# Third layer norm's factor in tile order and 36 two-operand operations on VectorE instead of GpSimd, in a float32 hybrid decoder block

## The chip, the cores and the metric

The kernel runs on one core of a Trainium2 chip, in one launch. The metric is the device time of that launch in microseconds (us), the median of several runs. Engines are named as in the profile: PE is TensorE (matmuls), DVE is VectorE, ACT is ScalarE, POOL is GpSimd, and SP issues the DMAs.

## What is computed

One layer on x of shape (1, 1024, 1024) in float32: a SwiGLU block with half weight, a token mixer (gated convolution beside an S5 state space), a second SwiGLU block, and a gated embedding, each followed by a layer norm.

```python
x = layer_norm(ALPHA * x + 0.5 * swiglu(x, ffn1_w_in, ffn1_w_out), ln1_g, ln1_b)
x = layer_norm(ALPHA * x + token_mixer(x, ...), ln2_g, ln2_b)
x = layer_norm(ALPHA * x + 0.5 * swiglu(x, ffn2_w_in, ffn2_w_out), ln3_g, ln3_b)
e = (p @ ple_w_in) * sigmoid(x @ ple_w_gate)
x = layer_norm(ALPHA * x + e, ln4_g, ln4_b)
```

Here `swiglu(x, w_in, w_out)` is `(silu(gate) * up) @ w_out` with `gate, up` the halves of `x @ w_in`; D is 1024, the inner width of a SwiGLU block 2816, the embedding 256 wide.

## The kernel before, in words

Every float32 product is made of three matmuls: an operand is split into a high part (a cast to fp32r on ACT, line 175) and a low part (operand minus high part, a two-operand instruction on DVE or POOL, line 176), and high times high, high times low and low times high are summed in PSUM (`pm` banks, six of them). Weights arrive in blocks of 128x512 (`Ws`), and their parts are `Wh` and `Wl`, three buffers each: PE can go on with a block when its `Wl` is written.

The large products are done with Winograd's variant of Strassen: seven products in place of eight. That needs sums of operands: of the activations (t1, t2, t3, t4 from the quarters 11, 12, 21, 22) once per stage, and of the weights for each pair of blocks (`rest`, lines 73 to 103; `s` is made by POOL at lines 79, 84 and 96).

Four places matter here.

- **The start.** `first_operands` (lines 380 to 439) loads x in pieces `xp` of 128x1024 and splits quarters 11 and 21. Its inner function `later` (lines 422 to 438) makes the activations' sums in two halves j = 0, 1: half 0 on DVE, half 1 on POOL, at lines 426, 429, 432 and 437. Each sum is then split (`xt1h`/`xt1l` and so on). Meanwhile PE does the first products of five block pairs (x11, then x21), then those on t1, t2, t3.
- **The two transitions into a Winograd stage**, from the first SwiGLU block into the mixer and from the mixer into the second SwiGLU block. `out_phase` (lines 219 to 237) does the output products (line 229) tile by tile, s = 0 to 7, DVE adds them into `acc` (line 234), and its callback `after(s)` normalizes the tile on DVE (`normalize`, `moments`, lines 241 to 265; the last step, line 265, for six of the eight) and, after every second tile, calls the sink on that pair of tiles. The sink transposes them on PE (line 281, into one of two `pt` banks), applies the norm's factor and offset on ACT (line 283) and makes and splits the sums (`winograd_sink`, lines 340 to 375): at lines 365, 369, 371 and 373 those of half j = 0 on POOL, of half j = 1 on DVE.
- **The transition into the last stage** has the same callback with `plain_sink` (lines 328 to 338), which only splits.
- **The last stage** (lines 1229 to 1259), tile by tile, s = 0 to 7. `apply(acc2[s])` (lines 311 to 316) multiplies a tile by the third norm's factor and adds its offset, columns 0 to 511 on DVE, columns 512 to 1023 on POOL, a product (line 315) and a sum (line 316) each, of 128x512. PE makes the gate's product (line 1243, 24 matmuls per half tile) into `pm` and the embedding's (line 1248, 6 matmuls) into `pt`. ACT takes the sigmoid (line 1251, `sg`), DVE multiplies the embedding's product by it (line 1252, which frees the `pt` bank), adds that to the tile (line 1253), and makes the last norm (lines 1254 to 1258), whose result goes out by DMA.

Who does what when is not written out: the program is recorded in the order of the code, and a scheduler then gives each engine its own queue, an instruction standing where it would have its inputs, earlier code first among those that are ready. Each engine then works through its queue in that order. `tc.issue_after(ins)`, which the change uses, holds what is recorded inside it behind `ins` in the queue of `ins`'s engine.

Of the kernel before, what the change touches and what calls it, by code (L numbers as in the profile page):

```python
# [12 lines left out]
ALU = mybir.AluOpType  # L13
P = 128
# [3 lines left out]
NT = 8  # L18
# [87 lines left out]
class Block:  # L106
# [112 lines left out]
    def out_phase(self, hs, ws, acc, scale, bank, after=None, fresh=False):  # L219
        nc = self.nc  # L220
        n = len(hs)
        for s in range(NT):
            for dh in range(2):
                ps = bank()
                cols = slice(dh * 512, (dh + 1) * 512)
                for j in range(n):
                    (hh, hl), (wh, wl) = hs[j], ws[j]
                    for i, (a, b) in enumerate(((hh, wh), (hh, wl), (hl, wh))):
                        nc.tensor.matmul(ps, a[:, s * P:(s + 1) * P], b[:, cols],  # L229
                                         start=(j == 0 and i == 0), stop=(j == n - 1 and i == 2))  # L230
                if fresh:
# [4 lines left out]
            if after is not None:  # L236
                after(s)

# [62 lines left out]
    def affine(self, g, b, tag):  # L301
# [8 lines left out]

        def apply(t):
            for h in range(2):
                sl = slice(h * 512, (h + 1) * 512)
                eng = (self.nc.vector, self.nc.gpsimd)[h]
                eng.tensor_tensor(t[:, sl], t[:, sl], gb[h], ALU.mult)
                eng.tensor_tensor(t[:, sl], t[:, sl], gb[2 + h], ALU.add)  # L316
        return apply
# [22 lines left out]
    def winograd_sink(self, xs, gb):  # L340
# [9 lines left out]
        def sink(i, pair):  # L350
# [8 lines left out]
            for j in range(2):  # L359
# [3 lines left out]
                self.features(pair, gb, 2 * j, b12)  # L363
                eng = (gps, self.nc.vector)[j]
                eng.tensor_tensor(t1, b12, b11, ALU.subtract)
# [14 lines left out]
    def first_operands(self, xT, w_in):  # L380
# [41 lines left out]
        def later():  # L422
            tt = [self.t("H", [P, 2, 512], name="t1") for _ in range(2)]
            eng = (nc.vector, nc.gpsimd)
            for j in range(2):
                eng[j].tensor_tensor(tt[j], p["12", j], p["11", j], ALU.subtract)
                put("t1", j, tt[j])
            for j in range(2):
                eng[j].tensor_tensor(tt[j], p["22", j], tt[j], ALU.subtract)
                put("t2", j, tt[j])  # L430
            for j in range(2):
                eng[j].tensor_tensor(p["12", j], p["22", j], p["12", j], ALU.subtract)
                put("t3", j, p["12", j])
            for j in range(2):
                put("22", j, p["22", j])
            for j in range(2):
                eng[j].tensor_tensor(tt[j], p["21", j], tt[j], ALU.subtract)
                put("t4", j, tt[j])
# [710 lines left out]
    def run(self, a, out):  # L1149
# [22 lines left out]
        def then(acc, make, sink):  # L1172

            state = {}

            def after(s):
                if s == 0:
                    state["x"] = make()
                    state["sink"] = sink(state["x"])
                self.normalize(acc[s], s < 2)  # L1180
                if s % 2:
                    state["sink"](s // 2, acc[s - 1:s + 1])
            return state, after
# [40 lines left out]
        for v in ("ln4_g", "ln4_b"):  # L1224
            for h in range(2):
                tl = self.t("Ws", [P, 512], name="gb4")
                nc.sync.dma_start(tl, a[v][h * 512:(h + 1) * 512].partition_broadcast(P))
                gb4.append(tl)
        for s in range(NT):
            cols = slice((s % 4) * P, (s % 4 + 1) * P)  # L1230
            if s % 2 == 0:
                pp = self.split_w(self.stage(a["pT"][:, s // 2]))
            apply(acc2[s])
            pcol = lambda k: slice((2 * (s % 2) + k) * P, (2 * (s % 2) + k + 1) * P)
            cuts = HALVES if s < NT - 1 else (slice(0, 512), slice(512, 768), slice(768, D))
            for sl in cuts:
# [14 lines left out]
                nc.scalar.activation(sg, pg, AF.Sigmoid)  # L1251
                nc.vector.tensor_tensor(sg, pe, sg, ALU.mult)
                nc.vector.scalar_tensor_tensor(acc2[s][:, sl], sg, 1.0 / ALPHA, acc2[s][:, sl], ALU.mult, ALU.add)
# [68 lines left out]
```

## Time and profile before

| | before |
|---|---|
| median of 3 runs | 2084.79 us (2083.38 to 2086.32) |
| the profiled execution, its own time | 2086.58 us |
| span of the profiled execution | 2084.8 us |
| PE busy | 2001.7 us, 96% of the span |
| DVE busy | 1668.0 us, 80% |
| ACT busy | 813.7 us, 39% |
| POOL busy | 846.4 us, 41% |
| mean granted clock of TensorE | 0.991 |

The span is the time from the first to the last instruction that the profile shows. PE is busy nearly all of it, and the share of an engine is a mean over stages of different kinds; what an edit is worth is read in the stage where it lies, from who waits there for whom. A matmul of 128x512 shows 0.39 us and the next one starts 0.227 us after it at the full clock, so 112 of them are seen in a stretch of 25 us that loses nothing.

### The profile page before, as it was taken

To read this page: it belongs to the slowest core of one execution; us is meant where nothing else is said; L and a number is where in the kernel's file an instruction comes from. 1 tells how busy PE (TensorE), PEld (TensorE's weight loads), DVE (VectorE), ACT (ScalarE), POOL (GpSimd) and SP (SyncE) were. 2 spreads that over 40 slices of the span, in tenths; PEclk is the share of its full clock that TensorE was granted. 3 is DMA by queue.
4 is the path that set the end of the run, shared out by engine and by line. 5 is a ranking of instruction groups with operands and counts; after the bars stand their busy time and mean duration, and the time that the engine had idled before them with its cause. 6 is when DMAs were issued, how large, how long until landed. Compare 5 with 4: busy or idle time off the path is not lost.

```text
span 2084.8 us, 26465 instructions
## 1 busy us (share of the span) xinstructions
PE 2001.7 (96%) x9030; PEld 1633.4 (78%) x9030; DVE 1668.0 (80%) x2560; ACT 813.7 (39%) x1422; POOL 846.4 (41%) x562
## 2 busy tenths in 40 slices
PE   7999999999999899999999999999999999999988
PEld 5887778776788777887878888788888876788867
DVE  7789888879998976767644679877667789998897
ACT  5333343445342545343533415533333345342520
POOL 3644444454313454333201372654444444313360
PEclk9999999999999999999999999999999999999999
DMA  4433343556540264333382410243323246431111
GB/s 170 127 117 96 122 141 126 179 186 223 164 141 25 106 187 148 100 122 114 133 299 80 151 53 17 83 149 117 101 87 126 91 166 217 162 128 69 54 45 69
DMA packets 153238, 260.24 MB, mean 125 GB/s; under 512 B 16144, under 2 KB 61200, under 8 KB 153104
## 3 DMA queue, kind: packets, MB, share of 16 engines
q1 hardware_dynamic: 153104, 258.56, 37.6%
q8 instruction: 71, 1.16, 0.2%
q14 instruction: 63, 0.52, 0.1%
HBM read 189.85 MB, written 68.65 MB: 124 GB/s over the span
## 4 chain that ended last, share of the span: by engine, by line
PE 67%; DVE 21%; issue 5%; DMA 2%; ACT 2%; POOL 2%; SPq 0%; DVEq 0%; POOLq 0%; ACTq 0%
PE pm L198 42%; PE pm L615 11%; PE pm L209 5%; PE pm L229 5%; DVE Wl L176 4%; PE pm L1243 2%; DVE wt L176 2%; DVE w L176 1%; DVE acc L622 1%; DVE ln L254 1%; PE pt L1248 1%; DVE ln L248 1%; DVE ln L255 1%; DVE acc L316 1%; DVE acc L234 1%
## 5 line engine op out<-in xcount | busy, mean ns | idle before, releaser
L175 ACT CAST Wh<-Ws 128x512 fp32r<-128x512 f32 x268 | 166.6, 622 | 346.5 <-PE pm L198 277.5
L176 DVE TENSOR_TENSOR Wl<-Ws,Wh 128x512 fp32r<-128x512 f32 x268 | 212.8, 799 | 109.1 <-ACT Wh L175 108.7
L175 ACT CAST Wh<-s 128x512 fp32r<-128x512 f32 x240 | 149.2, 622 | 379.2 <-PE pm L198 139.3
L176 DVE TENSOR_TENSOR Wl<-s,Wh 128x512 fp32r<-128x512 f32 x240 | 213.5, 890 | 25.8 <-ACT Wh L175 25.7
L615 PE MATMUL pm<-wt,Wh 128*128 128x512 f32 x640 | 188.0, 392 | 2.5 <-DVE acc L622 2.5
L84 POOL TENSOR_TENSOR s<-s,Ws 128x512 f32<-128x512 f32 x60 | 90.2, 1503 | 203.6 <-DVE Wl L176 193.3
L102 POOL TENSOR_TENSOR u<-u,p 128x512 f32<-128x512 f32 x60 | 96.1, 1602 | 144.3 <-DVE u L92 93.2
L615 PE MATMUL pm<-w,Wh 128*128 128x512 f32 x480 | 141.4, 392 | 6.1 <-ACT Wh L175 5.5
L622 DVE SCALAR_TENSOR_TENSOR acc<-pm,acc 128x512 f32<-128x512 f32 x200 | 132.7, 682 | 15.5 <-PE pm L615 14.8
L615 PEld LDWEIGHTS pm<-wt,Wh 128*128 128x128 f32 x640 | 119.7, 188 | 30.2 <-DVE acc L622 3.3
L79 POOL TENSOR_TENSOR s<-Ws 128x512 f32<-128x512 f32 x60 | 82.5, 1374 | 133.8 <-DVE Wl L176 102.0
L96 POOL TENSOR_TENSOR s<-Ws,s 128x512 f32<-128x512 f32 x60 | 92.3, 1538 | 108.8 <-DVE Wl L176 107.4
L615 PE MATMUL pm<-wt,Wl 128*128 128x512 f32 x320 | 113.8, 394 | 3.9 <-DVE Wl L176 3.6
L615 PEld LDWEIGHTS pm<-w,Wh 128*128 128x128 f32 x480 | 90.0, 189 | 26.8 <-ACT Wh L175 7.1
L198 PE MATMUL pm<-x11h,Wh 128*128 128x512 f32 (+1 forms) x264 | 99.1, 384 | 5.0 <-ACT x11h L175 5.0
L198 PE MATMUL pm<-x11h,Wl 128*128 128x512 f32 (+1 forms) x264 | 99.3, 379 | 3.1 <-DVE Wl L176 3.1
L198 PE MATMUL pm<-x11l,Wh 128*128 128x512 f32 (+1 forms) x264 | 99.6, 380 | 1.9 <-DVE x11l L176 1.3
L198 PE MATMUL pm<-xt1h,Wl 128*128 128x512 f32 x240 | 95.3, 397 | 5.3 <-DVE Wl L176 5.3
L198 PE MATMUL pm<-x21h,Wl 128*128 128x512 f32 x240 | 95.1, 396 | 5.5 <-DVE Wl L176 5.5
L198 PE MATMUL pm<-xt2h,Wl 128*128 128x512 f32 x240 | 94.8, 395 | 4.2 <-DVE Wl L176 4.1
L198 PE MATMUL pm<-xt4h,Wl 128*128 128x512 f32 x240 | 94.1, 392 | 4.6 <-DVE Wl L176 4.6
L198 PE MATMUL pm<-xt1l,Wh 128*128 128x512 f32 x240 | 94.4, 393 | 2.1 <-DVE xt1l L176 2.1
(355 smaller groups left out, 5615.7 us busy)
## 6 DMA issues: line engine op xcount, KB each, us to landing
Ws<-in_ffn_w_in SPq DMA_DIRECT2D x196, 256.0 KB, 2.7
Ws<-in_ffn_w_out SPq DMA_DIRECT2D x88, 256.0 KB, 3.1
Ws<-in_w_mix SPq DMA_DIRECT2D x74, 256.0 KB, 2.7
s<-h_s SPq DMA_DIRECT2D x60, 256.0 KB, 3.0
h<-a SPq DMA_DIRECT2D x58, 256.0 KB, 2.3
ha<-h SPq DMA_DIRECT2D x20, 512.0 KB, 4.1
hb<-h SPq DMA_DIRECT2D x20, 512.0 KB, 4.6
h_s<-u SPq DMA_DIRECT2D x20, 256.0 KB, 2.6
```

The costliest lines, as they stand in the source:

```text
L79: gps.tensor_tensor(s, a21, a22, ALU.add)
L84: gps.tensor_tensor(s, s, a11, ALU.subtract)
L96: gps.tensor_tensor(s, a12, s, ALU.subtract)
L102: gps.tensor_tensor(u3, u3, p5, ALU.add)
L175: self.nc.scalar.copy(hi, src)
L176: (lo_eng or self.nc.vector).tensor_tensor(lo, src, hi.bitcast(F32), ALU.subtract)
L198: self.nc.tensor.matmul(ps[:, tok], w[a][:, sl], x[b](k)[:, tok], start=(start and k == 0 and i == 0), stop=(k == nk - 1 and i == 2), skip ...
L209: self.nc.tensor.matmul(ps[h], w[a][:, sl], x(h)[b](k), start=(k == 0 and i == 0), stop=(k == 3 and i == 2))
L229: nc.tensor.matmul(ps, a[:, s * P:(s + 1) * P], b[:, cols], start=(j == 0 and i == 0), stop=(j == n - 1 and i == 2))
L615: nc.tensor.matmul(ps[i], hh[p][:, cols], w[n][:, j, q], start=(start and j == 0 and k == 0), stop=(j == 1 and k == 2), skip_group_check=n ...
L622: vec.scalar_tensor_tensor(t, ps[i], scale, t, ALU.mult, ALU.add)
L1243: nc.tensor.matmul(pg, xx[p](k % 4)[:, cols], wg[dh][k][q][:, col], start=(k == 0 and i == 0), stop=(k == NK - 1 and i == 2))
```

## The change

Four edits. The operands' sums of the start and of `winograd_sink` are all on DVE (4 + 16 instructions leave POOL). `apply` is on DVE alone (16 instructions leave POOL), and it is held, from the second tile on, behind the line 1252 instruction of the tile before. The sink of a pair of tiles is called one tile later, behind that tile's last output matmul on PE; the last pair's is called as before.

```diff
@@ out_phase
-                        nc.tensor.matmul(ps, a[:, s * P:(s + 1) * P], b[:, cols],
+                        mm = nc.tensor.matmul(ps, a[:, s * P:(s + 1) * P], b[:, cols],
...
-                after(s)
+                after(s, mm)
@@ affine
         def apply(t):
+            vec = self.nc.vector
             for h in range(2):
                 sl = slice(h * 512, (h + 1) * 512)
-                eng = (self.nc.vector, self.nc.gpsimd)[h]
-                eng.tensor_tensor(t[:, sl], t[:, sl], gb[h], ALU.mult)
-                eng.tensor_tensor(t[:, sl], t[:, sl], gb[2 + h], ALU.add)
+                vec.tensor_tensor(t[:, sl], t[:, sl], gb[h], ALU.mult)
+                vec.tensor_tensor(t[:, sl], t[:, sl], gb[2 + h], ALU.add)
@@ winograd_sink
-                eng = (gps, self.nc.vector)[j]
+                eng = self.nc.vector
@@ first_operands, later
-            eng = (nc.vector, nc.gpsimd)
+            vec = nc.vector
             for j in range(2):
-                eng[j].tensor_tensor(tt[j], p["12", j], p["11", j], ALU.subtract)
+                vec.tensor_tensor(tt[j], p["12", j], p["11", j], ALU.subtract)
...
@@ run, then
-            def after(s):
+            def after(s, mm):
...
                 self.normalize(acc[s], s < 2)
-                if s % 2:
+
+                if s % 2 == 0 and s:
+                    with self.tc.issue_after(mm.ins):
+                        state["sink"](s // 2 - 1, acc[s - 2:s])
+                elif s == NT - 1:
                     state["sink"](s // 2, acc[s - 1:s + 1])
@@ run, last stage
+        last = None
         for s in range(NT):
...
-            apply(acc2[s])
+
+            with self.tc.issue_after(last.ins) if last else ExitStack():
+                apply(acc2[s])
...
-                nc.vector.tensor_tensor(sg, pe, sg, ALU.mult)
+                last = nc.vector.tensor_tensor(sg, pe, sg, ALU.mult)
```

How the queues move, at three places. The names are those of the words above; a number is a buffer's.

On DVE at the start, from the sum for t1 on (`t_349` is half 0, `t_350` half 1), before:

```order
L426 TENSOR_TENSOR t_349<-xp 128x1024
L176 TENSOR_TENSOR Wl<-Ws,Wh 128x512
L176 TENSOR_TENSOR xt1l<-t_349,xt1h 128x1024
L176 TENSOR_TENSOR Wl<-Ws,Wh 128x512
L176 TENSOR_TENSOR xt1l<-t_350,xt1h 128x1024
L429 TENSOR_TENSOR t_349<-xp,t_349 128x1024
L432 TENSOR_TENSOR xp<-xp 128x1024
L176 TENSOR_TENSOR Wl<-Ws,Wh 128x512
L176 TENSOR_TENSOR xt2l<-t_349,xt2h 128x1024
L176 TENSOR_TENSOR Wl<-Ws,Wh 128x512
```

and now:

```order
L426 TENSOR_TENSOR t_349<-xp 128x1024
L176 TENSOR_TENSOR Wl<-Ws,Wh 128x512
L426 TENSOR_TENSOR t_350<-xp 128x1024
L176 TENSOR_TENSOR xt1l<-t_349,xt1h 128x1024
L176 TENSOR_TENSOR Wl<-Ws,Wh 128x512
L176 TENSOR_TENSOR xt1l<-t_350,xt1h 128x1024
L429 TENSOR_TENSOR t_349<-xp,t_349 128x1024
L432 TENSOR_TENSOR xp<-xp 128x1024
L176 TENSOR_TENSOR Wl<-Ws,Wh 128x512
L429 TENSOR_TENSOR t_350<-xp,t_350 128x1024
L432 TENSOR_TENSOR xp<-xp 128x1024
L176 TENSOR_TENSOR Wl<-Ws,Wh 128x512
```

The three sums of half 1 shown stand between the splits (the fourth, line 437, comes ten rows below); POOL's queue begins with line 79 instead.

On DVE at the beginning of the last stage (`acc_10364` to `acc_10371` are the tiles, `gb_16941` to `gb_16944` the two halves of the factor and of the offset), before, from the eighth product on:

```order
L315 TENSOR_TENSOR acc_10371<-acc_10371,gb_16941 128x512
L316 TENSOR_TENSOR acc_10364<-acc_10364,gb_16943 128x512
L316 TENSOR_TENSOR acc_10365<-acc_10365,gb_16943 128x512
L316 TENSOR_TENSOR acc_10366<-acc_10366,gb_16943 128x512
L1252 TENSOR_TENSOR sg_17057<-pt_17050,sg_17057 128x512
L316 TENSOR_TENSOR acc_10367<-acc_10367,gb_16943 128x512
L316 TENSOR_TENSOR acc_10368<-acc_10368,gb_16943 128x512
L1252 TENSOR_TENSOR sg_17093<-pt_17086,sg_17093 128x512
```

and now, from the first product on (lines are those of the changed kernel: 1252 is 1259 there, 1253 is 1260):

```order
L315 TENSOR_TENSOR acc_10364<-acc_10364,gb_16941 128x512
L315 TENSOR_TENSOR acc_10364<-acc_10364,gb_16942 128x512
L316 TENSOR_TENSOR acc_10364<-acc_10364,gb_16943 128x512
L1259 TENSOR_TENSOR sg_17057<-pt_17050,sg_17057 128x512
L316 TENSOR_TENSOR acc_10364<-acc_10364,gb_16944 128x512
L1260 SCALAR_TENSOR_TENSOR acc_10364<-sg_17057,acc_10364 128x512
L1259 TENSOR_TENSOR sg_17093<-pt_17086,sg_17093 128x512
L315 TENSOR_TENSOR acc_10365<-acc_10365,gb_16941 128x512
L315 TENSOR_TENSOR acc_10365<-acc_10365,gb_16942 128x512
```

Eleven products and sums, over eight tiles, stood ahead of the first line 1252 instruction; three of the first tile stand there now, and the other tiles' follow by turns.

On PE in the transition from the first SwiGLU block into the mixer, at the first transposes (line 281) among the output products, in the changed kernel:

```order
L229 MATMUL pm<-wo,hp 128x512 x43
L281 MATMUL pt<-ident,acc 128x128 x2
L229 MATMUL pm<-wo,hp 128x512 x26
L281 MATMUL pt<-ident,acc 128x128 x6
L229 MATMUL pm<-wo,hp 128x512 x8
L281 MATMUL pt<-ident,acc 128x128 x8
```

These rows are the same in the kernel before. Of each transition's 64 transposes, those of the first three pairs of tiles keep their places in PE's queue; those of the fourth pair move, in the two transitions into a Winograd stage, by up to 24 matmuls.

## Rows read from the trace of the kernel before

**Rows 1.** The page's part 1: engine, busy us, share, instructions.

```profile
PE 2001.7 (96%) x9030; PEld 1633.4 (78%) x9030; DVE 1668.0 (80%) x2560; ACT 813.7 (39%) x1422; POOL 846.4 (41%) x562
```

**Rows 2.** Windows: stretch, length; PE, PEld, DVE, ACT, POOL busy (instructions); clock; DMA, GB/s.

```profile
25.00:50.00 25.00, 18.18 (x64) 13.26 (x63) 25.00 (x16) 14.64 (x19) 15.32 (x6) 0.87 0.14 43
50.00:75.00 25.00, 25.00 (x112) 20.64 (x111) 16.13 (x21) 7.74 (x13) 15.52 (x11) 1.00 0.32 100
725.00:750.00 25.00, 21.07 (x89) 15.03 (x88) 24.41 (x25) 18.29 (x34) 16.16 (x11) 1.00 0.52 150
...
1300.00:1325.00 25.00, 20.95 (x91) 15.56 (x90) 21.31 (x23) 19.97 (x38) 18.37 (x10) 0.97 0.15 43
...
2000.00:2025.00 25.00, 17.70 (x61) 13.97 (x62) 24.93 (x33) 4.13 (x8) 15.88 (x10) 0.80 0.00 0
2025.00:2050.00 25.00, 25.00 (x112) 20.71 (x111) 24.97 (x70) 1.80 (x3) 0.00 (x0) 1.00 0.22 85
```

**Rows 3.** Instructions of one line: duration ns min/median/max, first and last start.

```profile
L365 DVE TENSOR_TENSOR t<-b,y x4: 677/682/687, 714.9 to 1317.0; 128x512 f32<-128x512 f32 x4
L365 POOL TENSOR_TENSOR t<-b,y x4: 1277/1527/1759, 708.1 to 1306.6; 128x512 f32<-128x512 f32 x4
```

**Rows 4.** The same view of line 315 in the last stage.

```profile
L315 DVE TENSOR_TENSOR acc<-acc,gb x8: 1684/1776/1780, 1986.1 to 1997.9; 128x512 f32<-128x512 f32 x8
```

**Rows 5.** Timeline of DVE at the start: start us, us, instruction, [idle before].

```profile
16.95 3.49 DVE L426 TENSOR_TENSOR t<-xp 128x1024 f32<-128x1024 f32 x1
...
24.65 1.22 DVE L429 TENSOR_TENSOR t<-xp,t 128x1024 f32<-128x1024 f32 x1
...
45.52 0.68 DVE L176 TENSOR_TENSOR Wl<-s,Wh 128x512 fp32r<-128x512 f32 x1
```

**Rows 6.** Timeline of POOL at the start.

```profile
46.27 2.19 POOL L84 TENSOR_TENSOR s<-s,Ws 128x512 f32<-128x512 f32 x1 [4.03 <-DVE Wl L176]
```

**Rows 7.** Timeline of PE at the start.

```profile
46.25 0.50 PE L198 MATMUL pm<-xt1h,Wl 128*128 128x512 f32 x1 [3.20 <-DVE Wl L176]
...
51.17 0.39 PE L198 MATMUL pm<-xt2h,Wl 128*128 128x512 f32 x1
```

**Rows 8.** Timelines of POOL, ACT and DVE in the two transitions into Winograd stages.

```profile
716.84 7.09 POOL L371 TENSOR_TENSOR t<-b,t 128x512 f32<-128x512 f32 x1 [3.84 <-DVE xt1l L176]
723.88 1.29 POOL L79 TENSOR_TENSOR s<-Ws 128x512 f32<-128x512 f32 x1
...
723.96 1.02 ACT L283 ACTIVATE b<-pt,gbT 128x256 f32<-128x256 f32 x2 [2.71 <-POOL t L371]
...
725.52 1.57 DVE L176 TENSOR_TENSOR Wl<-Ws,Wh 128x512 fp32r<-128x512 f32 x1 [2.74 <-ACT Wh L175]
...
1297.58 6.48 POOL L371 TENSOR_TENSOR t<-b,t 128x512 f32<-128x512 f32 x1 [5.07 <-DVE xt1l L176]
```

**Rows 9.** Waits of PE, us in total, times, longest: 715 to 750; then 1283 to 1345.

```profile
PE pm L198 <- DVE Wl L176: 3.5, 4, 1.4
...
PE pm L198 <- DVE Wl L176: 3.8, 3, 2.3
PE pm L198 <- DVE xt1l L176: 1.8, 1, 1.8
```

**Rows 10.** Timelines of DVE and PE at the beginning of the last stage.

```profile
1986.06 13.54 DVE L315 TENSOR_TENSOR acc<-acc,gb 128x512 f32<-128x512 f32 x8 [1.19 <-DMA gb<-in_ln_g]
1999.53 5.08 DVE L316 TENSOR_TENSOR acc<-acc,gb 128x512 f32<-128x512 f32 x3
2004.53 0.68 DVE L1252 TENSOR_TENSOR sg<-pt,sg 128x512 f32<-128x512 f32 x1
...
2005.27 1.22 PE L1248 MATMUL pt<-wp,Wh 128*128 128x512 f32 x2 [7.14 <-DVE sg L1252]
2016.14 1.07 PE L1248 MATMUL pt<-wp,Wh 128*128 128x512 f32 x2 [2.03 <-DVE sg L1252]
```

**Rows 11.** Groups of DVE from 2023 to 2050 us: busy us, mean ns.

```profile
L1257 DVE SCALAR_TENSOR_TENSOR acc<-acc,ln,gb 128x512 f32<-128x512 f32 x8 | 5.8, 743 | 0.0
```

More of the change, by code (lines that the diff above doesn't have):

```diff
@@ L228, in out_phase @@
                     for i, (a, b) in enumerate(((hh, wh), (hh, wl), (hl, wh))):
-                        nc.tensor.matmul(ps, a[:, s * P:(s + 1) * P], b[:, cols],
-                                         start=(j == 0 and i == 0), stop=(j == n - 1 and i == 2))
+                        mm = nc.tensor.matmul(ps, a[:, s * P:(s + 1) * P], b[:, cols],
+                                              start=(j == 0 and i == 0), stop=(j == n - 1 and i == 2))
                 if fresh:
@@ L423, in later @@
             tt = [self.t("H", [P, 2, 512], name="t1") for _ in range(2)]
-            eng = (nc.vector, nc.gpsimd)
+            vec = nc.vector
             for j in range(2):
-                eng[j].tensor_tensor(tt[j], p["12", j], p["11", j], ALU.subtract)
+                vec.tensor_tensor(tt[j], p["12", j], p["11", j], ALU.subtract)
                 put("t1", j, tt[j])
             for j in range(2):
-                eng[j].tensor_tensor(tt[j], p["22", j], tt[j], ALU.subtract)
+                vec.tensor_tensor(tt[j], p["22", j], tt[j], ALU.subtract)
                 put("t2", j, tt[j])
             for j in range(2):
-                eng[j].tensor_tensor(p["12", j], p["22", j], p["12", j], ALU.subtract)
+                vec.tensor_tensor(p["12", j], p["22", j], p["12", j], ALU.subtract)
                 put("t3", j, p["12", j])
@@ L436, in later @@
             for j in range(2):
-                eng[j].tensor_tensor(tt[j], p["21", j], tt[j], ALU.subtract)
+                vec.tensor_tensor(tt[j], p["21", j], tt[j], ALU.subtract)
                 put("t4", j, tt[j])
```

## The prediction, made before the changed kernel had run

> **What bounds the kernel now.** I read the shares first, then windows, then PE's waits, then timelines of whoever PE waits for. The shares show PE busy 96% of the span and POOL under half [rows 1]; PE decides, so only places where PE loses time count. A stretch of 25 us that loses nothing holds 112 full matmuls, one every 0.227 us (25/112). In the windows the reader should see four places that hold fewer [rows 2]: 64 at the start, 89 in the transition into the mixer, 91 in the next Winograd transition, 61 in the last stage; in all four DVE is busy 21 to 25 of 25 us. That is 10.9, 5.2, 4.8 and 11.6 us lost ((112 − n) × 0.227). All four are places of the change.
>
> Why is DVE late there? The same line and shape takes 0.68 us on DVE and 1.28 to 1.76 on POOL in a transition [rows 3], and 1.78 on DVE while POOL does the same work beside it [rows 4]. A 128x1024 sum takes 3.49 us beside POOL and 1.22 without [rows 5]. The two engines lengthen each other. Successive DVE instructions overlap by 0.08 us (eight shown as 13.54 us from 1986.06, the next at 1999.53 [rows 10]), so undisturbed ones cost **0.60** (512 columns) and **1.14** (1024).
>
> **The change, part by part.** Thirty-six instructions go from POOL to DVE: 4 of 1024 columns, 16 and 16 of 512. Undisturbed they add 4 × 1.14 + 32 × 0.60 = 23.8 us to DVE; the question is what the others get shorter by.
>
> *A, start.* PE's products on t1 wait 3.20 us, until 46.25, for the `Wl` that DVE writes last in a queue of splits and sums [rows 5, 7]. From the first sum (16.95) to the end of that `Wl` (46.2) DVE took 29.3 us. Its queue there, after the change, holds 15 instructions of 1024 columns and 6 of 512: 15 × 1.14 + 6 × 0.60 = 20.7 us. Three of the 15 are new, so the old queue was worth 17.3 and lost 12 us to POOL and to waits. POOL keeps two of the weights' sums in that time; one beside DVE took 2.19 [rows 6], and I let the pair cost DVE 2.2, with 1.1 for short waits: 16.95 + 24.0 = 41.0, 5.2 earlier. Three more instructions of 1024 (half 1 of t4, its splits) and three of 512 stand before t2's `Wl`: 41.0 + 3 × 1.14 + 3 × 0.60 = 46.2, where PE began t2's low part at 51.17 [rows 7]. **A = 5.0 us.** Low end 2, if POOL's remaining sums and waits take 6.5 in place of 3.3; high end 8.5, if neither costs anything (16.95 + 20.7 = 37.7). What is late next is PE itself, with the products on x21 still to do.
>
> *B, two Winograd transitions.* Eight sums each go to DVE, 8 × 0.60 = 4.8 us. Into the mixer POOL's t3 sum stood 7.09 us; ACT waited 2.71 for it, then DVE 2.74 for ACT's `Wh` [rows 8]: DVE, which PE waits for, was itself waiting for POOL. On DVE this sum costs 0.60 and the chain is gone, at 4.8 us of DVE work of which 2.74 fits in that wait. PE waited 3.5 us for `Wl` and lost 5.2 in the window [rows 9, 2]: **B1 = 3.5**, between 0 (the added work eats it) and 5.2. In the next transition the sum stood 6.48 [rows 8]; PE waited 3.8 for `Wl` and 1.8 for the t1 split [rows 9], 5.6 in all, at a granted clock of 0.97 in the window. **B2 = 4.5**, between 0.5 and 7 (the waits and the clock's loss). I take four fifths of the waits, since the late member of each chain moves to the engine PE waits for.
>
> *C, last stage.* The factor's pieces arrive by DMA at 1986; eleven products and sums then stand before the first line 1252 instruction, eight of them 13.54 us and three 5.08, and it starts at 2004.53. PE fills both `pt` banks and waits 7.14, later 2.03 [rows 10], and 112 − 61 gives 11.6 lost in that window, at a clock of 0.80 [rows 2]: some 9.2 of waits and 2.4 or more of matmuls at the lower of the clock's two levels (1.2 of 2.4 GHz) after each wait. From 1984 to 2045, by the same count, it is 14.3. After: three instructions of one tile stand ahead of the first release of a bank. The first piece is there at 1986; allowing 3 us until the others are, and 2 for the three instructions and the release itself, it comes near 1991 instead of 2005, before PE reached its wait (2005.27 − 7.14 = 1998.1). Steadily, DVE caught up four tiles in the 27 us of [rows 11] (two instructions each of line 1257 a tile): 6.75 us a tile without the factor, 6.75 + 4 × 0.60 = 9.2 with it. PE needs 60 × 0.227 = 13.6 a tile. DVE stays ahead and nothing waits. **C = 13**, between 9.5 (the waits alone, and little more) and 14.3.
>
> *The sinks one tile later: 0.* On PE the first three pairs' transposes keep their rows; the fourth moves by up to 24 matmuls, 24 × 0.227 = 5.4 us, covered by output products that are PE's work anyway. If uncovered this is a loss of up to 5.4 in each transition, within B's low end. The added wait on the matmul is one PE passes in its own order.
>
> Sum: 5.0 + 3.5 + 4.5 + 13 = **26 us**. Against the profiled execution: 2086.6 − 26 = 2060.6; it stood 1.8 above the median of the runs, so **2059**. All low ends give 12 (2072.8), all high 34.7 (2050).
>
> **A rule against it.** The trace has DVE full where PE waits, and the change adds work to it. The Trainium skill, "Perfetto Trace Analysis", section "Optimizing Scalar/DVE Operations", says that with DVE saturated it may make sense to hand work to GpSimd, and at once that this might not help since the two share a read port. By its first half the 23.8 us would come on top (the second rival below); [rows 4] against [rows 3], 1.78 against 0.68, are for its second half.
>
> **The rivals.**
>
> *1. POOL starves instead.* POOL keeps the sums of weights (lines 79, 84, 96), and DVE now works without gaps. What a POOL sum does behind a full DVE is the 7.09 and 6.48 us, against 1.29 for one just after [rows 8]. If the weights' sums take that place, each transition gives back about 5.5, and the start half of it, 2.8: 26 − 13.8 = 12, **2073**. For it: those rows, and the 4.03 POOL waited at the start [rows 6]. Against: those sums are made ahead, and the last stage has no such POOL work, so most of the gain is safe. The Trainium skill, "SBUF — State Buffer", section "Who interferes with whom", says that whoever issues first holds the shared port for its whole instruction and the other fully blocks, and that issue order decides; the 1.7 against 1.7 of the last stage (turns) and the 7.09 (starved) are both found in this trace. Chance 0.12.
>
> *2. DVE is the bound: slower.* If what lengthens DVE's rows is not POOL's sums but, say, what PE, ACT and the DMAs read at the same time, they stay long, and PE waits for `Wl` and banks while the added 23.8 us run: 2084.8 + 23.8 = **2108.6**. It decides where DVE per tile or block exceeds PE's: above 13.6 a tile in the last stage, which needs factor instructions of 1.7 each (6.75 + 6.8). For it: DVE's 24.4 to 25 of 25 us [rows 2]. Against: 0.68 for the same sum in the same busy transition [rows 3]. Chance 0.08, of which 0.03 for a mild form in which gains and cost cancel.
>
> *3. The order doesn't free banks in time.* If PE waits in every tile for its bank, because the factor now stands between the release of one and the next, C keeps only 4 of 13: **2068**. For it: DVE's 24.97 of 25 us even after the factor was done [rows 2]. Against: that was catching up. Chance 0.10.
>
> *4. Only the last stage pays.* The sums cost DVE in A and B what the contention did: 2084.8 − 13 = **2072**. Chance 0.10.
>
> **How the numbers follow.** The forecast has 0.60. The range 2050 to 2073 takes all bounds of the terms and rivals 1, 3 and 4; the second lies outside. About 0.2% (4 us) is what a measurement can tell here. Faster by more: 0.60 + 0.12 + 0.10 + 0.10 = 0.92; within it 0.03; slower 0.05.
>
> **What would show it.** Right: no DVE row of line 315 above 0.8 us; the first release of a `pt` bank (line 1259 now) near 1991 less what was gained earlier, no PE wait for it over 1 us, and 112 matmuls in each 25 us of the last stage; t1's first `Wl` product near 41 and t2's near 46; no wait of ACT for POOL in the transitions. Wrong: POOL rows of lines 79, 84 or 96 above 4 us with PE waiting behind them (rival 1); DVE rows still at 1.7 (2); PE waits of a few us per tile for line 1259 (3); PE's products on t1 still near 46 (4).

## The result and the profile after

The changed kernel takes **2061.79 us** (median of 4 runs, 2059.34 to 2064.03) against 2085.03 for the kernel before (4 runs). The ratio is 0.9889, with a 95% interval of 0.9872 to 0.9906: 23.2 us less, where 26 were forecast. The profiled execution took 2059.34, with a span of 2057.5.

The page's part 1 of the changed kernel:

```profile
PE 1992.3 (97%) x9030; PEld 1629.7 (79%) x9030; DVE 1646.9 (80%) x2596; ACT 812.5 (39%) x1422; POOL 795.8 (39%) x526
```

POOL has lost 36 instructions and 50.6 us of busy time. DVE has gained 36 instructions, and its busy time *fell* by 21.1 us [rows 1]: undisturbed they would cost 23.8 us by the prediction's price, so by this count DVE's other instructions got some 45 us shorter. That row shows the contention; what PE gets of it is read in its waits and its clock.

Where PE lost time before, the windows now read (stretch, length, then busy us and instructions of PE, PEld, DVE, ACT, POOL, clock, DMA share, GB/s):

```profile
25.00:50.00 25.00, 19.99 (x84) 15.08 (x84) 23.16 (x22) 16.00 (x22) 11.49 (x6) 1.00 0.23 61
...
725.00:750.00 25.00, 23.05 (x97) 17.43 (x96) 18.95 (x25) 13.62 (x24) 15.87 (x10) 1.00 0.73 221
...
1300.00:1325.00 25.00, 21.06 (x86) 16.55 (x84) 21.99 (x30) 12.47 (x24) 14.46 (x7) 0.93 0.20 63
...
1975.00:2000.00 25.00, 25.00 (x112) 20.70 (x111) 25.00 (x53) 5.18 (x9) 0.00 (x0) 1.00 0.00 1
```

Against [rows 2]: 84 matmuls for 64 at the start, 97 for 89 in the first Winograd transition, the full 112 in the last stage. The third row holds 86 where 91 stood, at a clock of 0.93; the program is 10 us further on there, so the window cuts another piece, but something is still lost in it.

The timelines of DVE, PE and POOL at the start (start us, us, instruction, what ended the idle time before it):

```profile
16.25 1.22 DVE L426 TENSOR_TENSOR t<-xp 128x1024 f32<-128x1024 f32 x1
...
39.60 0.68 DVE L176 TENSOR_TENSOR Wl<-s,Wh 128x512 fp32r<-128x512 f32 x1
...
40.33 0.50 PE L198 MATMUL pm<-xt1h,Wl 128*128 128x512 f32 x1 [3.24 <-DVE Wl L176]
44.39 0.50 PE L198 MATMUL pm<-xt2h,Wh 128*128 128x512 f32 x1 [1.45 <-ACT Wh L175]
...
40.36 3.33 POOL L84 TENSOR_TENSOR s<-s,Ws 128x512 f32<-128x512 f32 x1 [10.92 <-DVE Wl L176]
```

Three rows of PE before, and the one that stands now where the first of them stood:

```profile
32.06 0.50 PE L198 MATMUL pm<-x21h,Wl 128*128 128x512 f32 x1 [2.69 <-DVE Wl L176]
...
47.67 0.63 PE L198 MATMUL pm<-xt1h,Wh 128*128 128x512 f32 x1
48.09 0.63 PE L198 MATMUL pm<-xt1l,Wh 128*128 128x512 f32 x1
...
34.05 0.50 PE L198 MATMUL pm<-x21h,Wl 128*128 128x512 f32 x1 [0.31 <-DVE Wl L176]
```

The first sum fell from 3.49 to 1.22 us, and the `Wl` that PE waits for is done at 40.3 (forecast 41.0, before 46.2). PE waits as long as before for it [rows 7], since everything ahead came earlier too; POOL's second sum of weights is new in the chain (3.33 us, then ACT's cast, then 1.45 of PE). What went is the earlier wait for a `Wl` of the x21 products, 2.69 us then and 0.31 now. Behind t1's `Wl` little was gained up to t2: before, matmuls started 0.42 to 0.43 us apart there, at the lower level of the clock (0.50 from 47 to 50 us), and it was 3.98 us from 46.25 to the first product on t2; now they start about 0.23 apart, but with the 1.45 of waiting it is 4.06.

The timelines of POOL, ACT and PE in the two Winograd transitions, then PE's waits of [rows 9] as they are now (715 to 750, then 1283 to 1345):

```profile
715.79 11.31 POOL L79 TENSOR_TENSOR s<-Ws 128x512 f32<-128x512 f32 x1 [12.28 <-DVE Wl L176]
...
727.14 0.62 ACT L175 CAST Wh<-s 128x512 fp32r<-128x512 f32 x1 [3.07 <-PE pm L198]
...
1302.66 5.26 POOL L84 TENSOR_TENSOR s<-s,Ws 128x512 f32<-128x512 f32 x1 [4.24 <-DVE Wl L176]
...
1307.95 0.62 ACT L175 CAST Wh<-s 128x512 fp32r<-128x512 f32 x1 [4.11 <-POOL s L84]
...
1308.62 0.79 PE L198 MATMUL pm<-xt2h,Wh 128*128 128x512 f32 x1 [3.94 <-ACT Wh L175]
...
PE pm L198 <- DVE Wl L176: 1.1, 2, 0.6
...
PE pm L198 <- ACT Wh L175: 3.9, 1, 3.9
```

This is the first rival. The operands' sums of 7.09 and 6.48 us [rows 8] are gone from POOL, and POOL's sums of weights stand that long in their place, behind a DVE without gaps. In the first transition it is 11.31 us: ACT, which had been idle, casts the sum as soon as it is there (727.10), but PE still had other products to do, and its waits in that window come to 2.0 us in all (4.9 before). In the second a sum of 7.82 us (at 1288.89) makes PE wait nowhere, and one of 5.26 ends as a wait of PE.

The timeline of DVE and PE's waits at the beginning of the last stage (line 1259 was 1252; the waits are from 1965 us to the end of the matmuls):

```profile
1972.37 2.91 DVE L315 TENSOR_TENSOR acc<-acc,gb 128x512 f32<-128x512 f32 x2 [1.69 <-DMA gb<-in_ln_g]
1975.20 0.68 DVE L316 TENSOR_TENSOR acc<-acc,gb 128x512 f32<-128x512 f32 x1
1975.80 0.68 DVE L1259 TENSOR_TENSOR sg<-pt,sg 128x512 f32<-128x512 f32 x1
...
PE pm L1250 <- ACT sg L1258: 0.8, 1, 0.8
```

The first release of a bank comes 3.4 us after the factor's first piece; it was 18.5 [rows 10]. The waits of 7.14 and 2.03 us are gone. Of the 16 rows of line 315 the first two still took 1.23 and 1.76 us, beside two POOL splits (1971.75 to 1974.72); the others took 0.68 to 0.69.

### The profile page after: what moved, and what is told of

It reads as the page before. It is cut to its first block, busy times and chain, and to the rows that moved or that the text cites. A ratio compares the mean times of both kernels' runs of the same rounds, so it can differ in the third digit from the quotient of the medians.

```text
span 2057.5 us, 26438 instructions
## 1 busy us (share of the span) xinstructions
PE 1992.3 (97%) x9030; PEld 1629.7 (79%) x9030; DVE 1646.9 (80%) x2596; ACT 812.5 (39%) x1422; POOL 795.8 (39%) x526
## 4 chain that ended last, share of the span: by engine, by line
PE 70%; DVE 19%; issue 5%; DMA 2%; POOL 2%; ACT 1%; SPq 0%; DVEq 0%; POOLq 0%; ACTq 0%
PE pm L198 42%; PE pm L615 11%; PE pm L209 6%; PE pm L229 5%; DVE Wl L176 3%; PE pm L1250 3%; DVE wt L176 2%; DVE acc L622 2%; DVE w L176 2%; POOL s L79 1%; PE pt L1255 1%; DVE ln L254 1%; DVE ln L248 1%; POOL s L84 1%; DMA Ws<-in_ffn_w_out 1%
## 5 line engine op out<-in xcount | busy, mean ns | idle before, releaser
L176 DVE TENSOR_TENSOR Wl<-Ws,Wh 128x512 fp32r<-128x512 f32 x268 | 202.1, 759 | 103.5 <-ACT Wh L175 103.0
L79 POOL TENSOR_TENSOR s<-Ws 128x512 f32<-128x512 f32 x60 | 99.2, 1653 | 176.3 <-DVE Wl L176 113.1
L615 PEld LDWEIGHTS pm<-w,Wh 128*128 128x128 f32 x480 | 90.6, 190 | 24.9 <-ACT Wh L175 5.9
L198 PE MATMUL pm<-x11h,Wl 128*128 128x512 f32 (+1 forms) x264 | 99.2, 379 | 0.8 <-DVE Wl L176 0.8
L198 PE MATMUL pm<-xt2h,Wh 128*128 128x512 f32 x240 | 94.4, 393 | 5.4 <-ACT Wh L175 5.4
L198 PE MATMUL pm<-x22h,Wl 128*128 128x512 f32 x240 | 94.7, 395 | 0.9 <-DVE Wl L176 0.9
```

Of the source, the lines that this page charges most:

```text
L79: gps.tensor_tensor(s, a21, a22, ALU.add)
L176: (lo_eng or self.nc.vector).tensor_tensor(lo, src, hi.bitcast(F32), ALU.subtract)
L198: self.nc.tensor.matmul(ps[:, tok], w[a][:, sl], x[b](k)[:, tok], start=(start and k == 0 and i == 0), stop=(k == nk - 1 and i == 2), skip ...
L615: nc.tensor.matmul(ps[i], hh[p][:, cols], w[n][:, j, q], start=(start and j == 0 and k == 0), stop=(j == 1 and k == 2), skip_group_check=n ...
```

## The experiments

Beside the medians, four stretches are read from the starts of the rows of PE's matmuls in each kernel's timeline (a row can hold more than one), so that each place of the change is seen by itself (lines of the kernel before): **start**, from the first matmul to the first of line 868; **B1**, from the first of line 229 to the first of line 925; **B2**, from the last of line 209 to the last of line 198; **C**, from the first of line 1243 to the last of line 1248. Ratios are to the kernel before, run on the same chip.

| kernel | median, us | ratio (95%) | start | B1 | B2 | C |
|---|---|---|---|---|---|---|
| before | 2085.03 | | 212.4 | 105.4 | 526.0 | 131.0 |
| changed | 2061.79 | 0.9889 (0.9872 to 0.9906) | 205.8 | 101.9 | 522.2 | 117.8 |
| last_stage | 2073.45 | 0.9939 (0.9923 to 0.9954) | 211.4 | 105.6 | 525.8 | 117.7 |
| dve_no_order | 2073.63 | 0.9936 (0.9919 to 0.9952) | 211.1 | 105.3 | 525.9 | 117.9 |
| order_split | 2078.84 | 0.9961 (0.9948 to 0.9974) | 210.6 | 106.2 | 526.5 | 122.4 |
| order_both | 2083.56 | 0.9994 (0.9984 to 1.0003) | 212.0 | 106.4 | 525.9 | 127.4 |
| sums_only | 2075.05 | 0.9945 (0.9930 to 0.9960) | 206.1 | 101.7 | 523.1 | 131.2 |
| sinks_only | 2085.54 | 1.0003 (0.9994 to 1.0013) | 212.5 | 105.7 | 526.5 | 129.4 |
| engine_only | 2062.97 | 0.9890 (0.9874 to 0.9907) | 207.8 | 101.9 | 522.2 | 118.2 |
| after_again | 2063.00 | 0.9893 (0.9879 to 0.9908) | 206.5 | 101.9 | 522.8 | 117.9 |
| first_pair | 2054.70 | 0.9857 (0.9842 to 0.9871) | 204.5 | 99.2 | 519.4 | 117.9 |
| start_held | 2064.36 | 0.9902 (0.9886 to 0.9918) | 208.0 | 102.7 | 522.2 | 117.8 |
| pair_and_held | 2055.06 | 0.9856 (0.9841 to 0.9870) | 205.8 | 99.1 | 519.2 | 117.8 |
| pair_and_held2 | 2056.00 | 0.9861 (0.9843 to 0.9879) | 206.0 | 99.7 | 519.4 | 118.1 |

Kernels whose edit leaves a stretch alone show how far it moves by itself: the start 210.6 to 212.5, B1 105.3 to 106.4, B2 525.8 to 526.5, C (before, sums_only, sinks_only) 129.4 to 131.2.

### Each edit alone

**last_stage** is the kernel before with both edits of the last stage, engine and order:

```diff
+            vec = self.nc.vector
...
-                eng = (self.nc.vector, self.nc.gpsimd)[h]
...
-            apply(acc2[s])
...
+            with self.tc.issue_after(last.ins) if last else ExitStack():
+                apply(acc2[s])
...
+                last = nc.vector.tensor_tensor(sg, pe, sg, ALU.mult)
```

> The kernel before with the last stage's edit alone: the factor and offset on VectorE only, and in tile order. Theory (each edit pays in its own stage, and the gains add): about -13.3 us, what the trace of the changed kernel shows for this stage, so 2071 to 2072 us; PE waits for no release of a pt bank, the other three places read as before (64, 89 and 91 matmuls in their windows). Rival (the last stage's gain needs the earlier stages' shift, or the earlier gains were really the last stage's): under 8 us, or over 18 us.

The gain is 13.0 us (2086.41 before on that chip): C falls to 117.7 by itself, and the other stretches stay (the start's window holds 57 matmuls, not 64, at a clock of 0.73). **sums_only** is the complement, the operands' sums on DVE and nothing else:

```diff
-                eng = (gps, self.nc.vector)[j]
+                eng = self.nc.vector
...
-                eng[j].tensor_tensor(tt[j], p["12", j], p["11", j], ALU.subtract)
+                vec.tensor_tensor(tt[j], p["12", j], p["11", j], ALU.subtract)
...
```

> The kernel before with the operands' sums on VectorE alone (start and both Winograd transitions), nothing else. Theory: the shifts seen in the changed kernel's trace, 6 at the start, 3.5 in the transition into the mixer, 3.8 in the next, so -13 us, 2071 to 2072 us, with the last stage's wait of 7 us still there. Rival (sinks one tile later carry part of the transitions' gain): the transitions give under 4 together, gain of 6 to 10 us.

It gave 11.4 us, beside the same runs of before, where 13 were expected; its stretches are 6.3, 3.7 and 2.9 shorter, so all three places pay, and the second Winograd transition a little less than expected. In the last stage the waits of before stand unchanged (who waited for whom, us in total, times, longest; 1955 to 2050 us):

```profile
PE pt L1248 <- DVE sg L1252: 9.3, 2, 7.1
```

Together the two give 13.0 + 11.4 = 24.4 us, the whole change 22 to 23: the gains add, within the spread of the runs. **sinks_only** has the third edit alone:

```diff
-                if s % 2:
...
+                if s % 2 == 0 and s:
+                    with self.tc.issue_after(mm.ins):
+                        state["sink"](s // 2 - 1, acc[s - 2:s])
+                elif s == NT - 1:
                     state["sink"](s // 2, acc[s - 1:s + 1])
```

> The kernel before with the sinks called one tile later, behind the tile's last output matmul, and nothing else. Theory: within 1 us of the kernel before in each transition and in all, since PE's first three pairs of transposes keep their rows. Rival (the later sink gives room to the sums): 1 to 2 us gained in the second Winograd transition, where the whole change shows 3.7 us and the sums alone 2.9.

Nothing, in 10 runs against 19: 1.0003, and B1 and B2 within 0.5 us of before. The rival of this run falls.

### Order or engine, in the last stage

The prediction told the last stage as a matter of order: eleven instructions ahead of a release, three now. Three kernels take the edit apart. **order_split** has the tile order, and leaves the second half of each factor on POOL:

```diff
-            apply(acc2[s])
...
+            with self.tc.issue_after(last.ins) if last else ExitStack():
+                apply(acc2[s])
...
+                last = nc.vector.tensor_tensor(sg, pe, sg, ALU.mult)
```

> The kernel before with the tile order in the last stage alone; the second half of each factor stays on GpSimd. If the order is what frees the banks: VectorE has 1 or 2 products and sums ahead of the first release, at some 1.7 us each beside GpSimd, then per tile 6.75 + 2 x 1.7 = 10.2 us, still under PE's 13.6; gain 11 to 13 us, no wait of PE for a bank over 1 us. If the contention with GpSimd is what costs (engine theory): a gain of 0 to 6 us, with PE waits of several us for the release or for the tile halves that GpSimd makes.

It gave 7.6 us, between the ranges of the two theories, and C fell by 8.7. The hold acts on DVE's queue; POOL kept its own order, eight products, then eight sums, as its, DVE's and PE's timelines show:

```profile
1989.89 13.21 POOL L315 TENSOR_TENSOR acc<-acc,gb 128x512 f32<-128x512 f32 x8
...
2004.84 1.77 DVE L1256 SCALAR_TENSOR_TENSOR acc<-sg,acc 128x512 f32<-128x512 f32 x1 [1.19 <-POOL acc L316]
...
2014.55 0.68 DVE L1255 TENSOR_TENSOR sg<-pt,sg 128x512 f32<-128x512 f32 x1
...
2019.73 0.15 DVE L255 SCALAR_TENSOR_TENSOR ln<-ln 128x1 f32<-128x1 f32 x1
...
2015.28 1.22 PE L1251 MATMUL pt<-wp,Wh 128*128 128x512 f32 x2 [2.93 <-DVE sg L1255]
```

So the order was that of one engine alone, and **order_both** puts POOL in tile order as well:

```diff
+                with self.tc.issue_after(held[-1].ins) if held else ExitStack():
+                    self.nc.gpsimd.tensor_tensor(t[:, sl], t[:, sl], gb[h], ALU.mult)
+                    held.append(self.nc.gpsimd.tensor_tensor(t[:, sl], t[:, sl], gb[2 + h], ALU.add))
...
```

> The kernel before with the last stage in tile order on both engines: VectorE's half of a tile's factor held behind the release of a bank as in the change, GpSimd's half held behind its own sum for the tile before, so that GpSimd too goes tile by tile. The work is shared and lengthens on both sides as before. If order is what matters: the last stage takes 118 to 119.5 us from its first to its last matmul (131.0 before, 117.8 after the change, 122.4 with the order on VectorE's queue alone), a gain of 11 to 13 us. If the contention itself costs PE time: 121 us or more, a gain under 10.

Far from the 11 to 13 us: 0.8 us by the medians (by the interval between 3.3 faster and 0.6 slower), no difference from before that can be told. The profiled execution has C 3.6 us shorter; PE waits once, 7.57 us, in place of 7.14 and 2.03. The timelines of DVE, POOL and PE say why:

```profile
2001.28 0.68 DVE L1261 TENSOR_TENSOR sg<-pt,sg 128x512 f32<-128x512 f32 x1
...
2004.87 1.25 DVE L255 SCALAR_TENSOR_TENSOR ln<-ln 128x1 f32<-128x1 f32 x1
2006.04 0.68 DVE L176 TENSOR_TENSOR Wl<-Ws,Wh 128x512 fp32r<-128x512 f32 x1
2006.64 1.78 DVE L1262 SCALAR_TENSOR_TENSOR acc<-sg,acc 128x512 f32<-128x512 f32 x1
...
2010.05 0.68 DVE L248 BATCH_NORM_STATS2 ln<-acc 128x6 f32<-128x512 f32 x1
...
2016.32 0.68 DVE L1261 TENSOR_TENSOR sg<-pt,sg 128x512 f32<-128x512 f32 x1
...
2004.48 1.61 POOL L322 TENSOR_TENSOR acc<-acc,gb 128x512 f32<-128x512 f32 x1
...
2017.05 1.22 PE L1257 MATMUL pt<-wp,Wh 128*128 128x512 f32 x2 [7.57 <-DVE sg L1261]
```

An instruction of *one* column (line 255) takes 1.25 us: it begins at 2004.87 and ends at 2006.12, when POOL's sum ends (2004.48 + 1.61 = 2006.09). My price for this kernel had only the two factor instructions of a tile lengthened; in fact the norm's small steps and line 1262 are too. Between the releases at 2001.28 and 2016.32 stand 17 instructions that take 14.4 us; at their undisturbed prices (seven at 0.60, two of line 1266 at 0.67, eight short ones) they would take some 6.3, and the 8 us between is more than the wait of 7.57. With both engines in tile order and the contention kept, DVE falls behind all the same. order_split, with the same 16 instructions on POOL, kept 7.6 us: its tiles got POOL's sums later, so the norm's one-column steps of lines 254 and 255 came after POOL's last sum (2015.75), at some 0.15 to 0.2 us, and line 1255 came ahead of them. What an order is worth beside the contention therefore goes by what it puts into POOL's time. The Trainium skill, "SBUF — State Buffer", section "Who interferes with whom", states that a VectorE instruction with two inputs in SBUF contends with GpSimd's reads and that one with at most one such input, outside its two-port modes, does not; the trace agrees, with 0.68 for line 1261 (one input in PSUM) and line 248 (one input) beside POOL, against 1.78 for line 1262.

**dve_no_order** is the opposite half: the engine changed, the order left to the scheduler.

```diff
+            vec = self.nc.vector
...
-                eng = (self.nc.vector, self.nc.gpsimd)[h]
-                eng.tensor_tensor(t[:, sl], t[:, sl], gb[h], ALU.mult)
...
+                vec.tensor_tensor(t[:, sl], t[:, sl], gb[h], ALU.mult)
...
```

> The kernel before with the factor on VectorE alone in the last stage, not held in tile order: 16 products and sums stand ahead of the first release of a pt bank, 16 x 0.60 = 9.6 us, and 11 more ahead of the third. If the order is needed: PE still waits 3 to 6 us there, gain 4 to 9 us. If taking the contention away is enough by itself: the first release comes near 1997.5 instead of 2004.5, about when PE gets there (1998.1), the third near 2006 when PE needs it at 2012; gain 12 to 13.5 us, as with the order.

C is 117.9, the gain 12.8 us, as with the order. DVE's timeline and one window:

```profile
1985.54 11.20 DVE L315 TENSOR_TENSOR acc<-acc,gb 128x512 f32<-128x512 f32 x15 [1.22 <-DMA gb<-in_ln_g]
...
1997.27 0.68 DVE L1252 TENSOR_TENSOR sg<-pt,sg 128x512 f32<-128x512 f32 x1
...
1999.07 6.69 DVE L316 TENSOR_TENSOR acc<-acc,gb 128x512 f32<-128x512 f32 x11
...
2008.70 0.68 DVE L1252 TENSOR_TENSOR sg<-pt,sg 128x512 f32<-128x512 f32 x1
...
2000.00:2025.00 25.00, 25.00 (x111) 20.50 (x110) 25.00 (x57) 5.42 (x9) 0.00 (x0) 1.00 0.06 22
```

Sixteen instructions ahead of the first release now cost 11.7 us where eleven cost 18.5, and that is just early enough: the release at 1997.27 (expected 1997.5) precedes PE's need, and the third, at 2008.70, comes before the 2012 at which PE was expected there.

**engine_only** carries this to the whole kernel: all 36 instructions on DVE, no order, no later sinks. **after_again** is the changed kernel beside it.

> The kernel before with the engine changed and nothing else: the operands' sums and the last stage's factor on VectorE alone, the factor's instructions in the scheduler's own order, the sinks called as before. Theory (what pays is that GpSimd's two-operand instructions no longer run beside VectorE's; order and sinks carry nothing): within 2 us of the changed kernel run beside it, the last stage 118 us from its first to its last matmul, the start 6 us shorter, the two transitions 3 to 4 each. Rival (order needed once the earlier stages are faster, or the later sinks carry a part): 3 us or more slower than the changed kernel.

> The changed kernel itself, on the same chip as the two beside it, so that they can be compared: 2060 to 2063 us, and its stages as in its own trace within 1 us each.

2062.97 against 2063.00 us: of the four edits the two that move instructions do all the work, and the hold and the later sinks nothing that these runs can tell. engine_only's start is 207.8 us, 2 us longer than in the changed kernel, with the same wait (3.22 us) and a clock of 0.86 in the window from 25 to 50 us, where the changed kernel has 1.00.

### What is left: POOL's sums of weights

**first_pair** adds to the changed kernel the four sums of weights of the first block pair (lines 79, 84, 88, 96), in each of the three Winograd stages:

```diff
+        sums = vec if self.lead else gps
...
-        gps.tensor_tensor(s, a21, a22, ALU.add)
+        sums.tensor_tensor(s, a21, a22, ALU.add)
...
+        early[0].lead = True
```

Here `sums` is DVE for that pair and POOL for the others.

> The changed kernel, and the four sums of weights of the first block pair of each Winograd stage on VectorE too (12 instructions leave GpSimd). Theory (GpSimd starves behind a full VectorE, ACT's cast waits for its sum, PE for the cast): the 5.26 us of GpSimd's second sum and PE's wait of 3.94 us in the second Winograd transition go, 3 to 4 us gained there; 0.5 to 1 us in the transition into the mixer; 0 to 2 at the start; together 3.5 to 6 us below the changed kernel, near 2057. Rival (VectorE is full there, and 12 more instructions delay its own splits): no gain, PE's waits turn into waits for Wl from VectorE, within 1.5 us of the changed kernel or slower.

More than expected: 2054.70 us, and against the changed kernel the start is 1.3 to 2 us shorter, B1 2.7 (0.5 to 1 expected), B2 2.8 to 3.4. So POOL's starved sums had cost something in the first transition too. PE's waits from 1283 to 1345 us, where one of 3.9 us for ACT's cast stood:

```profile
PE pm L199 <- DVE Wl L177: 0.4, 1, 0.4
PE pm L199 <- ACT Wh L176: 0.4, 1, 0.4
```

So the chain of the first rival was real, and its remedy is the change's own, carried further. This kernel is the fastest of the study, level with pair_and_held below (0.9856); its interval (0.9842 to 0.9871) lies clear of that of after_again.

The start still has a wait of 3 us for the first `Wl`, behind splits that are needed later. **start_held** (on the changed kernel), **pair_and_held** (on first_pair) and **pair_and_held2** hold the splits of quarter 22 and the sums for t4 behind that `Wl`, or, the last, behind the next:

```diff
+        if self.hook is not None:
+            with blk.tc.issue_after(blk.lo.ins):
+                self.hook()
```

> The changed kernel, and at the start the splits of quarter 22 and the sums for t4 held behind the split of the first weights' sum on VectorE, which they stood ahead of (the sum L437, two splits of x22, 3.4 us). Theory (that queue is what makes PE wait 3.24 us for the products on t1): the wait goes, 2.5 to 4 us gained by the first matmul of line 868, none elsewhere; near 2058.5. Rival (ACT's cast or the later operands come last there): under 1 us gained at the start, a wait of PE for x22 or t4 in its place.

> The changed kernel with the first pair's sums of weights on VectorE and the start's quarter 22 and t4 held behind the split of the first weights' sum. Theory (holding alone failed because GpSimd's second sum then starved behind a VectorE without gaps, 5.58 us, and PE waited 3.75 us for ACT's cast of it; with that sum on VectorE the starvation is gone): the start falls by 2 to 3.5 us against the first pair alone (204.46 to the first matmul of line 868), no PE wait over 1 us on t1 or t2; near 2052. Rival (the order at the start is bound by ACT's casts): within 1 us of the first pair alone, 2054 to 2055.

> The kernel pair_and_held with the start's quarter 22 and t4 held behind the split of the second weights' sum (for t2) in place of the first: behind the first, PE's wait moved from t1 to t2, 3.49 us in place of 3.01 and 1.02, because the second weights' sum stood behind the held splits. Theory (PE waits for what stands last in VectorE's queue, and only t1 and t2 are needed early): neither product waits over 1 us, the time to the first matmul of line 868 falls from 204.5 to 201.5 to 203 us, near 2052.5. Rival (the start is bound by VectorE's work as a whole, so the wait moves on to x22 or t4): 204 us or more, 2054 to 2055, with a wait of 2 us or more for x22 or t4.

All three missed. In start_held the wait for t1 went, and POOL's next sum starved behind the DVE that had been closed up, as POOL's and PE's timelines show:

```profile
36.99 5.58 POOL L87 TENSOR_TENSOR s<-s,Ws 128x512 f32<-128x512 f32 x1 [7.51 <-DVE Wl L179]
...
43.27 0.79 PE L201 MATMUL pm<-xt2h,Wh 128*128 128x512 f32 x1 [3.75 <-ACT Wh L178]
```

With that sum on DVE (pair_and_held) it stood behind the held splits instead, and PE's timeline has the same wait at the same place:

```profile
40.87 0.79 PE L202 MATMUL pm<-xt2h,Wh 128*128 128x512 f32 x1 [3.49 <-ACT Wh L179]
```

Held one step later (pair_and_held2), the wait is cut in two and moves on to t3 and x22:

```profile
42.98 0.50 PE L202 MATMUL pm<-xt3h,Wl 128*128 128x512 f32 x1 [1.50 <-DVE Wl L180]
48.66 0.79 PE L202 MATMUL pm<-x22h,Wl 128*128 128x512 f32 x1 [1.84 <-DVE Wl L180]
```

The start takes 204.5 us with the first pair alone, 205.8 and 206.0 with the holds. PE's waits did not get longer: from 25 to 50 us they come to 4.0 us with the first pair alone and to 3.5 and 3.3 with the holds. pair_and_held began the products on t2 at 40.87 us, 1.35 ahead of first_pair, and those on x22 at 49.33, 1.42 behind it, since the matmuls between ran at the lower level of the clock. In start_held it is the same: t2 at 43.27 for the changed kernel's 44.39, x22 at 51.44 for 50.09. The window from 25 to 50 us of first_pair, then of pair_and_held:

```profile
25.00:50.00 25.00, 20.98 (x91) 16.46 (x91) 23.66 (x27) 15.83 (x22) 3.97 (x3) 1.00 0.28 77
...
25.00:50.00 25.00, 21.51 (x82) 16.88 (x81) 21.61 (x25) 15.47 (x22) 3.26 (x2) 0.86 0.26 75
```

So the holds moved PE's waits and shortened them a little, and the clock, 1.00 against 0.86, took back more than that (in pair_and_held2 it is 0.97, and 0.96 in the next 25 us). What else bounds the start was not tried.

## Why the prediction was right

The forecast held in sign and size: 2059 for 2061.79 us, inside 2050 to 2073. By terms, with the stretches of the table (the mean of the kernels that leave the stretch as before, less the mean of changed, after_again, engine_only and, for A and B, sums_only):

| term | forecast, us | measured, us |
|---|---|---|
| A, start | 5.0 | 211.7 − 206.5 = 5.1 |
| B1 | 3.5 | 105.75 − 101.83 = 3.9 |
| B2 | 4.5 | 526.0 − 522.6 = 3.4 |
| C, last stage | 13 | 130.5 − 118.0 = 12.5 |

Their sum, 24.9, is some 2 us more than the medians give (22 to 23); the stretches are single profiled executions, and that rest, about the spread of the runs, is not explained.

- **The mechanism.** Right: the contention between two-operand instructions on both engines was what DVE lost, and 23.8 us of added work came back nearly twice over (45 us). What PE gained were shorter waits and, at the start and in the last stage, a clock that fell less often; the sum had priced the clock in C (2.4 us or more) and not in A. The second rival, DVE's rows staying long, fell with the page's first row.
- **A.** Right, and nearly to the row: the first `Wl` at 40.3 for 41.0, POOL's remaining cost included (the two DVE rows from 25.96 us on took 1.1 us more each beside it, for 2.2 forecast), and t2's low part at 45.47 for 46.2. PE's wait there did not shrink, though; the whole queue moved forward, so "what is late next is PE itself" was wrong. DVE stayed late. Two things behind that `Wl` stand nowhere in the sum: the wait of 1.45 us behind POOL's second sum, and the clock, which from 25 to 50 us lay between 0.73 and 0.93 in the six kernels that leave the start alone, and at 1.00 in three of the four that change it (0.86 in engine_only, whose start is the longest of the four). That they about cancel was luck.
- **B1** came out at 3.9 for 3.5. The four fifths that the prediction says it takes of the waits stand in B2 alone (5.6 × 0.8); B1 takes its 3.5 us of waits for `Wl` whole.
- **B2** was mis-sized by 1 us. The step that failed is the sentence that the chain is gone: it was the old chain that went, and a new one of the first rival's kind, POOL's second sum of weights, 5.26 us, gave PE a new wait of 3.94 us. What the prediction listed as a sign of being right, no wait of ACT for POOL in the transitions, did not hold (4.11 us). The first rival's price of 5.5 at each transition was too high, but not nothing in either: taking the first pair's sums off POOL (first_pair) gave 2.7 us in the first transition and 2.8 to 3.4 in the second. Its counter-argument, that those sums are made ahead, held in part.
- **C** was right in size, and its reason was half wrong. The sum was built on the order, three instructions ahead of a release in place of eleven; dve_no_order shows that the engine without the order gives it all, and the order with the contention left gives 7.6 us (order_split) or nothing that can be told (order_both). So the order was one way to an earlier release, and not needed once the engine had changed. The first sign, no row of line 315 above 0.8 us, held for 14 of 16 rows. Also, DVE's 9.2 us a tile against PE's 13.6 overstated the margin: 144 of the 408 gate matmuls lay ahead of 1970 us, so the eight tiles came in the 78 us that were left, some 9.8 us each, and DVE was full for 25 us from the factor's arrival on (25.00 in the window from 1975 us). The third rival's condition was nearer than its chance said, but PE had no wait.
- **The sinks, 0.** Right (sinks_only).
- **The range.** The high ends add up to 35.0, not 34.7, and 25/112 is 0.223; the step of 0.227 us is the one that the trace shows. Neither moves the forecast.

## What to carry to other kernels

Two engines that lengthen each other's instructions do not add up: before work is split between VectorE and GpSimd, compare one row of the same instruction with and without the other engine beside it (here 0.68 against 1.78 us, and 1.22 against 3.49), and price the split by what it does to everything else in the queue, down to the one-column steps. When instructions are taken off GpSimd, look at once at what GpSimd still does in that stretch, since a VectorE without gaps starves it; here it paid another 7 to 8 us to put the sums that come first in a stage on the same engine as the rest. A new order in a queue is to be tested apart from the edit it came with: here it gave nothing beside the change of engine, and 0 to 8 us without it. And where a stage's gain is counted, look at the granted clock of its windows as well as at the waits.

## What the runs showed of the hardware that was not expected

- A one-column VectorE instruction took 1.25 us beside a GpSimd sum, against 0.15 in stretches where GpSimd rests: the step ended when GpSimd's instruction ended, so the loss went by that and not by VectorE's own size.
- A GpSimd sum of 128x512 stood up to 11.31 us behind back-to-back VectorE work, for 1.29 undisturbed.
- The granted clock fell after some waits and not after others of the same length. From 25 to 50 us it was 0.86 with a single wait of 3.49 us (pair_and_held, 82 matmuls) and with 3.22 and 0.55 (engine_only, 77), and 1.00 with 3.24 and 1.45 (changed, 84) and with 3.01 and 1.02 (first_pair, 91). What decided it was not settled; so a wait's price is more than its length in some executions.
